# In feed-forwards x on the other side of the weights, 64 bytes off, and three gate units with weights at 256-byte multiples from x

## The chip, the core and the metric

The kernel runs on one core of a Trainium2 chip. The metric is the device time of one execution in microseconds (us). One execution was also taken with the hardware profiler; all rows below come from that one.

## What is computed

Two transformer blocks on 256 positions of width 1024, all in float32, one after the other. The first has a mixer (a gated delta rule and an S5 state space), a cross-attention and a SwiGLU feed-forward. The second has two layers, each with a self-attention (stick-breaking and MoBA heads in layer 0, forgetting attention in layer 1), a cross-attention to a memory, and a feed-forward with a short convolution over the positions. So there are three feed-forwards, of this form:

```python
def _swiglu(x, w_gate, w_up, w_down):
    return (silu(x @ w_gate) * (x @ w_up)) @ w_down      # 1024 -> 2816 -> 1024
def conv_ffn(h, w_up, conv_w, conv_b, w_down):
    c = conv_b + sum(up[:, i:i + S] * conv_w[i] for i in range(3))   # up = h @ w_up, padded in front
    return (silu(c[..., :2816]) * c[..., 2816:]) @ w_down
```

## The kernel before

**Products.** A float32 product is made of three products of rounded halves (mm3, and the same in out_mm): weight high by x high, weight high by x low, weight low by x high. The weights are the stationary operand (128x128, an LDWEIGHTS), x is the moving one (128x256), except in the V projections (proj_t), where x is stationary and the weights move. A unit of weights is 128x1024 numbers: 24 matmuls, 8 slices by three products.

**Weights.** The class Weights holds all units in the order of their use. load_ahead (L101) loads each from HBM into a raw tile. pump takes the next unit: ACT writes its rounded half into whi (L137) and, at the next pump, DVE writes the rest into wlo (L157). There are four pairs of whi and wlo tiles in the pool "weights", and from the first feed-forward on three more in the pool "weights2" (W.more). A unit takes one of the four if one is free, else one of the three, and gives it back when its last matmul has read it. So at most seven units are split at a time. step calls pump(1) after each unit of matmuls.

**Feed-forward.** ffn runs over 22 column blocks j: the gate unit (g), the up unit (u), and, two or three blocks later (LAG), the down unit (d) of an earlier block. Unit 0 of a feed-forward is g of j=0, so that g of j=8 is the 23rd unit used with LAG 2 and the 22nd with LAG 3. The last four down units are used together at the end. In the first feed-forward, "f0", rope_consts is called at j=4; it has one tiny matmul on TensorE (L1809). residual makes the next x out of the accumulated sums: it writes N.xh and N.xl, tiles of 8 slices of 256 numbers, sl and ahl hold the down product's moving operand, and N.rb a row scale that the readers of a projection multiply by.

**Addresses.** Tiles lie one behind the other in a partition's memory, pool behind pool. As laid out before, every whi and wlo tile starts 192 bytes behind a multiple of 256 (the first at byte 24,000), xh, xl and ahl 128 bytes behind one (xh at byte 69,248). A weight slice takes 512 bytes and a slice of x 1024, so the distance between two operands modulo 256 is the same for all slices. In what follows the **distance** of a matmul is the start of its moving operand minus the start of its stationary one, modulo 256. It is -64 for all products of a unit of weights with x, ahl or an attention's output as the moving operand. It is +64 in the V projections, where the roles are exchanged. It is 0 in the S5 gate (s5ghl by whi) and in the scores and the application of the first cross-attention (V, lb and K by Q, PT by xvh). These three are all that occur in long runs.

The tile v1 (192 bytes, at the start of the pool "main"), "beside" (128 bytes) and "beside2" (64 bytes) set these offsets.

Of the kernel before, what the change touches and what calls it, by code (L numbers as in the profile page):

```python
# [10 lines left out]
F32 = mybir.dt.float32  # L11
F32R = mybir.dt.float32r
# [7 lines left out]
S = 256  # L20
KD = D // 128
# [11 lines left out]

MEMORY = "s0 w1 s1 w1 s2 w1 s3 w1 v0 t0 w1 v1 t1 w1 p0 t2 w1 p1 x0 t3 w1 p2 p3 x1".split()

XK_AT = [("v", 1), ("z", 0), ("z", 1), ("z", 1)]
EPS = 1e-6
PI = math.pi
# [6 lines left out]
class Weights:  # L45
# [3 lines left out]
    def __init__(self, nc, pool, nraw, nsplit, behind):  # L49
        self.nc, self.pool, self.nraw, self.nsplit = nc, pool, nraw, nsplit  # L50
        self.plan, self.units, self.gain, self.gains = {}, [], {}, None
        self.loaded = 0
        self.raw, self.place, self.parts, self.where = {}, {}, {}, {}
        self.lo = self.more = None
        self.next = 0

        self.extra, self.nextra, self.once, self.spares, self.live = None, 0, False, [], {}
        self.lane = lambda k: nullcontext()
        self.hold, self.held, self.behind = None, 0, behind
# [53 lines left out]
    def pump(self, n=1):  # L113

        for _ in range(n):
            while self.next < self.loaded and not self.plan[self.units[self.next][0]][2]:
                self.next += 1
            if self.next >= len(self.units) or len(self.where) >= self.nsplit + (self.more[1] if self.more else 0):
                self.finish_lo()
                return False  # L120
            if self.next >= self.loaded:
                self.finish_lo()
            if self.next >= self.loaded:
                return False
            u = self.units[self.next]
            src = self.raw[u]
            shape = [128, int(src.shape[1]), int(src.shape[2])]
            used = list(self.where.values())
            at = int(used.count(0) == self.nsplit)
            pool, tag, bufs = (self.more[0], "2", self.more[1]) if at else (self.pool, "", self.nsplit)  # L130
            hi = pool.tile(shape, F32R, name="whi", tag="whi" + tag, bufs=bufs)
            lo = pool.tile(shape, F32R, name="wlo", tag="wlo" + tag, bufs=bufs)
            self.where[u] = at
            with self.lane("w"):
                g = self.gain[u[0]]
                if g is None:
                    i_ = self.nc.scalar.activation(hi, src, AF.Copy)  # L137
                else:
                    for k in range(shape[1]):
                        n = u[1] * shape[1] + k  # L140
                        i_ = self.nc.scalar.activation(hi[:, k], src[:, k], AF.Copy, scale=self.gains[g][:, n:n + 1])
            if self.held > 0:
                self.behind(i_.ins, self.hold[0])
            self.finish_lo()
            self.lo = (lo, src, hi, u)
            self.parts[u] = (hi, lo)
            self.next += 1
        return True
# [81 lines left out]
def body(ctx, tc, I, out):  # L230
# [5 lines left out]
    const = ctx.enter_context(tc.tile_pool(name="const", bufs=1))  # L236
    wpool = ctx.enter_context(tc.tile_pool(name="weights", bufs=1))
    main = ctx.enter_context(tc.tile_pool(name="main", bufs=1))
    small = ctx.enter_context(tc.tile_pool(name="small", bufs=2))
    W = Weights(nc, wpool, 4, 4, lambda a, b: behind(tc, a, b))  # L240

    v1 = main.tile([128, 48], F32, name="v1")


    def cols(w, c0, c1):
# [23 lines left out]
            W.order((nm, int(x[1])), c)  # L269

    def plan_ffn(tag, wg, g0, wu, u0, wd):
        for p in range(NH // 2):
            W.add((tag, "g", p), cols(wg, g0 + 256 * p, g0 + 256 * p + 256), order=False)
            W.add((tag, "u", p), cols(wu, u0 + 256 * p, u0 + 256 * p + 256), order=False)
            W.add((tag, "d", p), rows(wd, 2 * p), "k", order=False)
        lag = LAG[tag]
        for j in range(NH + lag):
            for c, jj in (("g", j), ("u", j), ("d", j - lag)):
                if 0 <= jj < NH:
                    W.order((tag, c, jj // 2), jj % 2)  # L280
# [115 lines left out]
    COL = W.gains = {}  # L396
# [64 lines left out]
    N = State()  # L461
# [1 line left out]
    N.by_feature = True  # L463
    N.last = None

    def new_x():
        N.xh = main.tile([128, KD, S], F32R, name="xh", tag="xh", bufs=1)
        N.xl = main.tile([128, KD, S], F32R, name="xl", tag="xl", bufs=1)

    def split_x(n, src, gcol):  # L470
        a = A.activation(N.xh[:, n], src[:, n], AF.Copy, scale=gcol)
# [5 lines left out]
    def finish_r(v):  # L477

        exp = A.set == A.SETS[AF.Exp]
        e = V if not late1 else A if exp or not N.by_feature else G  # L480
        late1.append(1)
        N.r = rsqrt_small(v, 2, e)
        if not N.by_feature:
            return
        p = acc()
        bcast_rows(p, N.r, 2)
        N.rb = main.tile([128, S], F32, name="rb", tag="rb", bufs=2)
        V.tensor_copy(N.rb, p[:, :S])

    def sum_rows(p, c0, sq):  # L490
# [92 lines left out]
        T.matmul(p, lhsT=wh[:, kk, c], rhs=xl, start=False, stop=False, skip_group_check=True)  # L583
        T.matmul(p, lhsT=wl[:, kk, c], rhs=xh, start=False, stop=last, skip_group_check=True)  # L584

    def residual(accs, gcol, fold=None, by_feature=True):


        h = hn = N.h
        N.by_feature = by_feature  # L590
        new_x()
        if fold is not None:
            gg = small.tile([128, KD], F32, name="gg", tag="gg", bufs=1)
            V.tensor_tensor(gg, gcol, fold, op=OP.mult)
            gcol = gg
# [28 lines left out]
        def first():  # L624
            p = acc()
# [15 lines left out]
            N.r = rr[:, 0:2]  # L641
            p = acc()
            bcast_rows(p, rr, 4)
            N.rb = main.tile([128, S], F32, name="rb", tag="rb", bufs=2)
            V.tensor_copy(N.rb, p[:, :S])

            def normed():
# [54 lines left out]

    N.h = hT = main.tile([128, KD, S], F32, name="h", tag="h", bufs=1)
    new_x()
    def transpose_in(dst, src, evac, bank):
        for kp in range(4):
            p = bank()
            pv = halves(p)
            for k2 in range(2):
                for t in range(2):  # L710
                    k = 2 * kp + k2
                    T.transpose(pv[:, k2, t * 128:(t + 1) * 128], src[t][:, k * 128:(k + 1) * 128], ident)
            evac(kp, pv)
# [8 lines left out]
    for n in range(KD):  # L722
        src, gcol = xb[n // 2][:, n % 2], COL["mix"][:, n:n + 1]
# [663 lines left out]
    for n in range(4):  # L1387
        p = mm()
# [5 lines left out]
        if n == 1:  # L1394
            split_x32()
        W.pump(1)
    fin_v(lambda i, n: v1[:, 0:n] if i else const.tile([128, n], F32, name="v0"))
    layer_cols()
    mixed = []

# [118 lines left out]


    pm = ctx.enter_context(tc.tile_pool(name="second", bufs=1))
    pm.tile([128, 32], F32, name="beside")
    kvT = pm.tile([128, 2, S], F32, name="kvT")
    kvv = pm.tile([128, 2, S], F32, name="kvv")

# [154 lines left out]
    for x in CROSS:  # L1680
        ops[x[0]](int(x[1]))
    mem2l = w_["mem2l"]
    residual(accs, COL["ffn"])
    px_cm.__exit__(None, None, None)
    W.more = (ctx.enter_context(tc.tile_pool(name="weights2", bufs=1)), 3)
    W.more[0].tile([128, 16], F32, name="beside2")
    padded = ctx.enter_context(tc.tile_pool(name="padded", bufs=1))
    W.nextra = 2
    W.extra = lambda: main.tile([128, 2048], F32, name="raw4", tag="m8", bufs=3)
# [20 lines left out]
    def ffn(tag, gcol, conv=None, fold=None):  # L1710
# [12 lines left out]
        def act(j, p):  # L1723
# [18 lines left out]
            s = pm.tile([128, S], F32, name="sl", tag="e3", bufs=6)  # L1742
            A.activation(s, t[:, 0], AF.Silu)
            tt(s, s, t[:, 1], OP.mult)
            a = pm.tile([128, 2, S], F32R, name="ahl", tag="e3", bufs=6)
            st.last = A.activation(a[:, 0], s, AF.Copy, keep=True).ins
            tt(a[:, 1], s, a[:, 0].bitcast(F32), OP.subtract)
            st.a[j] = (a[:, 0], a[:, 1])
# [270 lines left out]
    def memory_attention(l, gcol):  # L2019
# [39 lines left out]
            ops[x[0]](int(x[1]))  # L2059
        accs = [acc() for _ in range(4)]  # L2060
        out_last(accs, ("xao", l), w["o"], True)
        residual(accs, gcol)

    def fox_gates():

# [120 lines left out]
```

## Time and profile before

| | |
|---|---|
| median of 3 runs | 1190.58 us (1190.51 to 1200.14) |
| the profiled execution's own time | 1196.38 us |
| its span, first to last instruction | 1194.6 us |
| TensorE (PE) busy in it | 97% |
| VectorE (DVE), ScalarE (ACT) | 75%, 56% |

The time of an execution is its span and under 2 us around it. The busy share of PE is made of modelled ends, so it tells that PE is hardly ever without work, not how fast it works; how fast is read from the number of matmuls in a stretch.

### The profile page before, as it was taken

Reading aid. Unit: us, or ns where it says so; the run is one execution under the profiler, and the core shown is the slowest. Engines: PE = TensorE matmul, PEld = TensorE weight load, DVE = VectorE, ACT = ScalarE, POOL = GpSimd, SP = SyncE. Lnnn points to the kernel's source line nnn. Section 1 sums busy time; section 2 is a strip of 40 time slices with the busy share of each in tenths; the row PEclk is TensorE's granted clock in tenths of the full one; section 3 lists DMA queues with packets and bytes.
Section 4 is the critical chain, followed back from the end, with each engine's and each line's share of the span. In section 5 each row is a group of like instructions: output and inputs, shape, how many; then the busy total and the mean of one; then the engine's idle time right before and its main releaser. Section 6 shows DMA issues by size and latency. Waiting matters only on the chain.

```text
span 1194.6 us, 24101 instructions
## 1 busy us (share of the span) xinstructions
PE 1156.8 (97%) x9720; PEld 1102.7 (92%) x9720; DVE 891.8 (75%) x1682; ACT 667.1 (56%) x1155; POOL 77.1 (6%) x175
## 2 busy tenths in 40 slices
PE   8999998999999999999998999999999999999998
PEld 6798888999999999988797999999988888999998
DVE  8899747866875565877876899877765686978775
ACT  6553345655644444756665665655454666655653
POOL 1425300100000000200000000000100000000000
PEclk9999899999999999999999999999999999999998
DMA  8733352746665665653353576665543464666530
GB/s 207 198 83 109 98 159 63 220 150 188 194 198 169 195 198 163 185 169 118 105 168 113 162 208 194 195 212 158 145 140 116 143 172 137 179 190 195 176 90 36
DMA packets 262017, 188.01 MB, mean 157 GB/s; under 512 B 20143, under 2 KB 246852, under 8 KB 261906
## 3 DMA queue, kind: packets, MB, share of 16 engines
q1 hardware_dynamic: 258034, 185.23, 52.9%
q8 instruction: 76, 1.25, 0.4%
q10 hardware_dynamic: 3568, 0.86, 0.3%
q0 software_dynamic: 304, 0.39, 0.3%
q14 instruction: 35, 0.29, 0.1%
HBM read 183.70 MB, written 2.75 MB: 156 GB/s over the span
## 4 chain that ended last, share of the span: by engine, by line
PE 83%; DVE 7%; DMA 4%; ACT 2%; issue 1%; POOL 1%; SPq 0%; ACTq 0%; DVEq 0%; POOLq 0%
PE mm L536 16%; PE mm L537 16%; PE mm L538 16%; PE acc L582 7%; PE acc L584 7%; PE acc L583 7%; DVE wlo L157 1%; PE acc L1995 1%; DMA raw<-in_w_in_dram 1%; DVE s5a L747 1%; DVE ca L1110 1%; PE acc L1866 1%; DMA s5u<-uT 1%; DMA raws<-in_w_out_dram 1%; ACT whi L137 1%
## 5 line engine op out<-in xcount | busy, mean ns | idle before, releaser
L157 DVE TENSOR_TENSOR wlo<-raw,whi 128x1024 fp32r<-128x1024 f32 x322 | 392.0, 1226 | 149.6 <-ACT whi L137 147.3
L137 ACT ACTIVATE whi<-raw 128x1024 fp32r<-128x1024 f32 x322 | 337.0, 1057 | 285.6 <-PE mm L537 106.2
L536 PE MATMUL mm<-xh,whi 128*128 128x256 f32 x1504 | 421.3, 281 | 2.3 <-ACT V L218 1.4
L537 PE MATMUL mm<-xl,whi 128*128 128x256 f32 x1504 | 420.1, 280 | 0.0
L538 PE MATMUL mm<-xh,wlo 128*128 128x256 f32 x1504 | 419.7, 279 | 0.0
L536 PEld LDWEIGHTS mm<-xh,whi 128*128 128x128 f32 x1504 | 283.4, 189 | 4.3 <-ACT V L218 1.5
L537 PEld LDWEIGHTS mm<-xl,whi 128*128 128x128 f32 x1504 | 282.8, 188 | 1.5 <-issue 1.0
L538 PEld LDWEIGHTS mm<-xh,wlo 128*128 128x128 f32 x1504 | 283.6, 189 | 0.3
L584 PE MATMUL acc<-ahl,wlo 128*128 128x256 f32 x528 | 144.8, 279 | 0.4 <-DVE wlo L157 0.4
L583 PE MATMUL acc<-ahl,whi 128*128 128x256 f32 x528 | 144.9, 279 | 0.0
L582 PE MATMUL acc<-ahl,whi 128*128 128x256 f32 x528 | 141.7, 279 | 0.2 <-ACT ahl L218 0.2
L584 PEld LDWEIGHTS acc<-ahl,wlo 128*128 128x128 f32 x528 | 99.2, 189 | 0.8 <-DVE wlo L157 0.8
L583 PEld LDWEIGHTS acc<-ahl,whi 128*128 128x128 f32 x528 | 98.9, 188 | 0.0
L582 PEld LDWEIGHTS acc<-ahl,whi 128*128 128x128 f32 x528 | 97.2, 189 | 0.5 <-ACT ahl L218 0.5
L1740 DVE SCALAR_TENSOR_TENSOR gu<-pad,cwc,gu 128x256 f32<-128x256 f32 x176 | 75.1, 478 | 3.4 <-ACT gu L218 3.4
L582 PE MATMUL acc<-oh,whi 128*128 128x256 f32 x224 | 61.8, 284 | 0.9 <-ACT oh L218 0.9
L584 PE MATMUL acc<-oh,wlo 128*128 128x256 f32 x224 | 61.9, 279 | 0.0
L583 PE MATMUL acc<-ol,whi 128*128 128x256 f32 x224 | 61.7, 278 | 0.0
L218 ACT ACTIVATE gu<-pad,cwc 128x256 f32<-128x256 f32 x88 | 47.5, 590 | 14.7 <-DVE pad L747 14.6
L582 PEld LDWEIGHTS acc<-oh,whi 128*128 128x128 f32 x224 | 41.3, 188 | 2.5 <-ACT oh L218 1.9
L584 PEld LDWEIGHTS acc<-oh,wlo 128*128 128x128 f32 x224 | 42.1, 188 | 1.1 <-issue 1.1
L583 PEld LDWEIGHTS acc<-ol,whi 128*128 128x128 f32 x224 | 42.2, 188 | 0.4 <-issue 0.4
(537 smaller groups left out, 1951.7 us busy)
## 6 DMA issues: line engine op xcount, KB each, us to landing
raw<-in_ffn_w_up_dram SPq DMA_DIRECT2D x88, 512.0 KB
raw<-in_ffn_w_down_dram SPq DMA_DIRECT2D x44, 512.0 KB
raw<-in_ab_w_in_dram SPq DMA_DIRECT2D x24, 512.0 KB
raw<-in_fox_w_in_dram SPq DMA_DIRECT2D x24, 512.0 KB
raw<-in_w_gate_dram SPq DMA_DIRECT2D x22, 512.0 KB
raw<-in_w_up_dram SPq DMA_DIRECT2D x22, 512.0 KB
raw<-in_w_down_dram SPq DMA_DIRECT2D x22, 512.0 KB
raw<-in_w_in_dram SPq DMA_DIRECT2D x20, 512.0 KB
```

Source lines behind the costliest of these rows:

```text
L137: i_ = self.nc.scalar.activation(hi, src, AF.Copy)
L157: i_ = self.nc.vector.tensor_tensor(lo, src, hi.bitcast(F32), op=OP.subtract)
L218: i = self.nc.scalar.activation(out, in_, func, **kw)
L536: T.matmul(p, lhsT=wh, rhs=xh, start=start, stop=False, **kw)
L537: T.matmul(p, lhsT=wh, rhs=xl, start=False, stop=False, **kw)
L538: T.matmul(p, lhsT=wl, rhs=xh, start=False, stop=stop, **kw)
L582: T.matmul(p, lhsT=wh[:, kk, c], rhs=xh, start=first and n % 2 == 0, stop=False, skip_group_check=True)
L583: T.matmul(p, lhsT=wh[:, kk, c], rhs=xl, start=False, stop=False, skip_group_check=True)
L584: T.matmul(p, lhsT=wl[:, kk, c], rhs=xh, start=False, stop=last, skip_group_check=True)
L747: N.v = V.tensor_tensor(o, a, b, op=op).ins
L1110: STT(a, c[:, i:i + S], w(i), a, op0=OP.mult, op1=OP.add)
L1740: STT(t[:, i], u[:, i, d:d + S], cw(d, j + NH * i), t[:, i], op0=OP.mult, op1=OP.add)
```

## The change

Six parts, in the order of the diff.

- **Slots.** W.more now has two ordinary pairs instead of three, and a seventh pair (tag "3") that only the gate units of j = 1, 3 and 8 (APART) of each feed-forward take, when it is free. Two gaps of 64 bytes lie ahead of the two and ahead of the one.
- **x in one tile.** xh and xl are two parts of one tile of 16,384 + 128 bytes. The residuals ahead of the three feed-forwards put them 128 bytes further on (at=32), all others at its start.
- **ahl** likewise lies 128 bytes further on in its tile.
- **rb** has one buffer instead of two.
- **v1** goes from main to const, and a gap of its size stays in main. So everything from the weights on lies 192 bytes further on, weights and x alike.
- "gap1" (128 bytes) fills up what the 128 bytes of x's tile left of 256; "beside" is now "gap2".

By these sizes the distance of all products of a feed-forward becomes +64 instead of -64, apart from the nine APART gate units, where it is 0. Outside the feed-forwards all distances of products with weights stay as they were.

```diff
+APART = (1, 3, 8)
@@ pump
-            if self.next >= len(self.units) or len(self.where) >= self.nsplit + (self.more[1] if self.more else 0):
+            used = list(self.where.values())
+            if self.next >= len(self.units):
                 self.finish_lo()
                 return False
+            if self.more and self.units[self.next] in self.apart and 2 not in used:
+                at = 2
+            else:
+                at = int(used.count(0) == self.nsplit)
+                if at and (not self.more or used.count(1) == self.more[1]):
+                    self.finish_lo()
+                    return False
...
-            at = int(used.count(0) == self.nsplit)
-            pool, tag, bufs = (self.more[0], "2", self.more[1]) if at else (self.pool, "", self.nsplit)
+            pool = self.more[0] if at else self.pool
+            tag, bufs = (("", self.nsplit), ("2", 2), ("3", 1))[at]
@@ body
-    v1 = main.tile([128, 48], F32, name="v1")
+    main.tile([128, 48], F32, name="gap")
@@ plan_ffn
+        W.apart.update(((tag, "g", j // 2), j % 2) for j in APART)
...
-    def new_x():
-        N.xh = main.tile([128, KD, S], F32R, name="xh", tag="xh", bufs=1)
-        N.xl = main.tile([128, KD, S], F32R, name="xl", tag="xl", bufs=1)
+    def new_x(at=0):
+        t = main.tile([128, 2 * KD * S + 32], F32R, name="x", tag="x", bufs=1)
+        N.xh, N.xl = (t[:, at + i * KD * S:at + (i + 1) * KD * S].rearrange("p (k s) -> p k s", k=KD) for i in range(2))
...
-        N.rb = main.tile([128, S], F32, name="rb", tag="rb", bufs=2)
+        N.rb = main.tile([128, S], F32, name="rb", tag="rb", bufs=1)
...
-    def residual(accs, gcol, fold=None, by_feature=True):
+    def residual(accs, gcol, fold=None, by_feature=True, at=0):
...
-        new_x()
+        new_x(at)
...
+    main.tile([128, 32], F32, name="gap1")
...
-    fin_v(lambda i, n: v1[:, 0:n] if i else const.tile([128, n], F32, name="v0"))
+    fin_v()
...
-    residual(accs, COL["ffn"])
+    residual(accs, COL["ffn"], at=32)
     px_cm.__exit__(None, None, None)
-    W.more = (ctx.enter_context(tc.tile_pool(name="weights2", bufs=1)), 3)
-    W.more[0].tile([128, 16], F32, name="beside2")
+    W.more = (ctx.enter_context(tc.tile_pool(name="weights2", bufs=1)), 2)
+    W.more[0].tile([128, 16], F32, name="gap3")
+    for n in ("whi", "wlo"):
+        for i in range(2):
+            W.more[0].tile([128, 1024], F32R, name=n, tag=n + "2", bufs=2)
+    W.more[0].tile([128, 16], F32, name="gap4")
@@ act
-            a = pm.tile([128, 2, S], F32R, name="ahl", tag="e3", bufs=6)
+            a = pm.tile([128, 2 * S + 32], F32R, name="ahl", tag="e3", bufs=6)[:, 32:].rearrange("p (i s) -> p i s", i=2)
@@ memory_attention
-        residual(accs, gcol)
+        residual(accs, gcol, at=32)
```

## Rows read from the trace of the kernel before

**Rows 1.** The span and granted TensorE clock; busy time, share and instructions by engine.
```profile
core 0: 1194.6 us, clock 0.987
PE 1156.8 (97%) x9720; PEld 1102.7 (92%) x9720; DVE 891.8 (75%) x1682; ACT 667.1 (56%) x1155; POOL 77.1 (6%) x175
```

**Rows 2.** The chain that ended last, its shares of the span by engine.
```profile
PE 83%; DVE 7%; DMA 4%; ACT 2%; issue 1%; POOL 1%; SPq 0%; ACTq 0%; DVEq 0%; POOLq 0%
```

**Rows 3.** Windows, us from:to, length, busy (instructions) by engine; feed-forwards one, two, three.
```profile
336.00:480.00 144.00, 144.00 (x1223) 144.00 (x1224) 89.67 (x119) 65.31 (x91) 0.00 (x0) 1.00 0.61 181
670.00:826.00 156.00, 156.00 (x1377) 155.86 (x1376) 131.84 (x212) 93.65 (x144) 0.93 (x1) 1.00 0.66 193
1026.00:1177.00 151.00, 151.00 (x1284) 150.96 (x1282) 119.62 (x192) 85.86 (x130) 0.00 (x0) 1.00 0.52 156
```

**Rows 4.** Groups of matmuls in 336:480, then in 670:826; us busy, mean ns.
```profile
L536 PE MATMUL mm<-xh,whi 128*128 128x256 f32 x272 | 76.4, 281 | 0.0
...
L536 PE MATMUL mm<-xh,whi 128*128 128x256 f32 x303 | 83.6, 276 | 0.0
```

**Rows 5.** PE in order of time, 181.6 to 184: distance 0; first and last of 20.
```profile
181.64 0.28 PE L536 MATMUL mm<-s5ghl,whi 128*128 128x256 f32 x1
...
183.92 0.28 PE L536 MATMUL mm<-s5ghl,whi 128*128 128x256 f32 x1
```

**Rows 6.** Windows right behind distance 0, at distance -64.
```profile
243.90:249.50 5.60, 5.60 (x50) 5.60 (x49) 4.60 (x10) 2.99 (x8) 0.00 (x0) 1.00 0.63 187
258.50:264.10 5.60, 5.60 (x50) 5.60 (x49) 3.42 (x8) 2.26 (x5) 0.00 (x0) 1.00 0.43 134
```

**Rows 7.** Windows: V projections, distance +64, begun after a break on PE.
```profile
519.30:524.50 5.20, 5.20 (x46) 5.20 (x46) 5.16 (x12) 1.45 (x2) 0.00 (x0) 1.00 0.27 81
```

**Rows 8.** Windows: distance -64, then +64 without a break.
```profile
495.00:498.70 3.70, 3.70 (x35) 3.70 (x35) 3.70 (x4) 2.41 (x5) 1.90 (x2) 1.00 0.62 180
499.00:502.70 3.70, 3.70 (x35) 3.70 (x34) 2.69 (x4) 1.86 (x3) 1.82 (x2) 1.00 0.81 226
```

**Rows 9.** PE in order of time at 335.4: the tiny matmul of rope_consts.
```profile
335.61 0.38 PE L1809 MATMUL mm<-ones,invrow 1*128 1x1 f32 x2
```

**Rows 10.** Windows: the three feed-forwards in parts.
```profile
336.00:363.00 27.00, 27.00 (x230) 27.00 (x231) 20.99 (x35) 12.72 (x20) 0.00 (x0) 1.00 0.59 184
366.00:480.00 114.00, 114.00 (x970) 114.00 (x970) 66.94 (x83) 51.22 (x69) 0.00 (x0) 1.00 0.62 182
320.00:335.00 15.00, 15.00 (x135) 15.00 (x134) 10.91 (x18) 7.79 (x14) 1.59 (x33) 1.00 0.74 221
652.00:663.00 11.00, 11.00 (x99) 11.00 (x99) 9.47 (x16) 7.84 (x13) 0.00 (x0) 1.00 0.18 53
672.00:826.00 154.00, 154.00 (x1360) 153.86 (x1358) 129.96 (x210) 93.47 (x143) 0.93 (x1) 1.00 0.66 192
998.00:1008.00 10.00, 10.00 (x91) 10.00 (x90) 8.81 (x15) 6.89 (x12) 0.00 (x0) 1.00 0.17 52
1016.00:1025.00 9.00, 9.00 (x82) 9.00 (x81) 8.50 (x15) 5.78 (x10) 0.00 (x0) 1.00 0.33 99
1026.00:1057.00 31.00, 31.00 (x265) 30.98 (x264) 27.10 (x48) 18.47 (x30) 0.00 (x0) 1.00 0.73 223
1060.00:1176.00 116.00, 116.00 (x987) 116.00 (x987) 89.40 (x140) 64.69 (x96) 0.00 (x0) 1.00 0.47 141
```

**Rows 11.** What PE waited for, whole span: the one wait for a split.
```profile
PE acc L584 <- DVE wlo L157: 0.4, 1, 0.4
```

**Rows 12.** Groups of the splits; us busy, mean ns, idle before.
```profile
L157 DVE TENSOR_TENSOR wlo<-raw,whi 128x1024 fp32r<-128x1024 f32 x322 | 392.0, 1226 | 149.6 <-ACT whi L137 147.3
L137 ACT ACTIVATE whi<-raw 128x1024 fp32r<-128x1024 f32 x322 | 337.0, 1057 | 285.6 <-PE mm L537 106.2
```

More of the change, by code (lines that the diff above doesn't have):

```diff
@@ L54, in __init__ @@
         self.lo = self.more = None
+        self.apart = set()
         self.next = 0
@@ L127, in pump @@
             shape = [128, int(src.shape[1]), int(src.shape[2])]
-            used = list(self.where.values())
-            at = int(used.count(0) == self.nsplit)
-            pool, tag, bufs = (self.more[0], "2", self.more[1]) if at else (self.pool, "", self.nsplit)
+            pool = self.more[0] if at else self.pool
+            tag, bufs = (("", self.nsplit), ("2", 2), ("3", 1))[at]
             hi = pool.tile(shape, F32R, name="whi", tag="whi" + tag, bufs=bufs)
@@ L643, in first @@
             bcast_rows(p, rr, 4)
-            N.rb = main.tile([128, S], F32, name="rb", tag="rb", bufs=2)
+            N.rb = main.tile([128, S], F32, name="rb", tag="rb", bufs=1)
             V.tensor_copy(N.rb, p[:, :S])
@@ L1521, in body @@
     pm = ctx.enter_context(tc.tile_pool(name="second", bufs=1))
-    pm.tile([128, 32], F32, name="beside")
+    pm.tile([128, 32], F32, name="gap2")
     kvT = pm.tile([128, 2, S], F32, name="kvT")
```

## The prediction

> **What bounds the kernel now.** I read the shares by engine first: PE is busy 97% of the span, at a granted clock of 0.987 [rows 1]. The chain that ended last says the same: 83% of it is PE, no other engine over 7% [rows 2]. PE waited once, for 0.4 us, for a split of weights [rows 11]. So the time is the number of matmuls times the time from one start to the next, and that is read by counting matmuls in a stretch.
>
> The three feed-forwards do this in long unbroken runs, and not at one pace [rows 3]. In the first, 1223 matmuls take 144 us: 117.7 ns each. In the second, 1377 take 156 us: 113.3 ns. In the third, 1284 take 151 us: 117.6 ns. The granted clock is 1.00 in all three, the 2.4 GHz level, so the clock isn't the difference. The kind of matmul isn't either: it is the same line, with the same operands at the same distance (-64), and the records show 281 ns in one run and 276 in the other [rows 4]. I call the two **slow** and **fast**. They differ by 4.4 ns a matmul, and each holds for over 1200 matmuls, through gate, up and down products. A break on PE can change it: at 335.6 us a tiny matmul comes between [rows 9], the stretch ahead of it is fast (15 us, 135 matmuls) and that behind it slow [rows 10]. So the same program can run each feed-forward at either pace. One whole feed-forward is worth some 1377 x 4.4 = 6.1 us, close to what lies between the profiled execution (1196.38) and the median (1190.58).
>
> **What the traces show of the distance.** At distance 0 there is one pace only: 19 steps from 181.64 to 183.92 are 120 ns each [rows 5]. At -64 and at +64 both paces occur, and changing from -64 to +64 without a break keeps a run fast (35 matmuls in 3.7 us on both sides) [rows 8]; in the trace this holds 7 times of 7 for fast, 3 of 3 for slow. What a run comes out of decides its pace. Out of distance 0 into -64 without a break it was slow 9 times of 9, if more than two matmuls stood at 0 (5.6 us for 50 matmuls, two or three of them cut by the window's edges) [rows 6]. Out of a break into -64 it was fast 41 times and slow 24 times. Out of a break into +64 it was slow 15 times of 16 (46 matmuls in 5.2 us) [rows 7]. Distance 0 into +64 does not occur in the trace. That is the step on which this change hangs.
>
> **The change part by part.** Sum against the profiled execution's own 1196.38 us.
>
> *Distance +64 in feed-forwards.* By itself it gains nothing: pace is carried over, and out of a break it is worse than -64, slow rather than fast. I count all matmuls of a feed-forward ahead of the first clean passage through distance 0 as slow. The g unit of j=1 is used mixed with those of j=0, so I take j=3 as the first clean one (321, 669 and 1018 us). In the second feed-forward 99 matmuls from 652 to 663 turn slow, in the third 91 from 998 to 1008 [rows 10]: 190 x 4.4 = **0.8 us lost**. The first was mostly slow there.
>
> *Nine units at distance 0.* 216 matmuls at 120 ns. Where the run was fast, 6.7 ns more each, where it was slow, 2.3: the first feed-forward has one of three in a fast stretch, the second all three, the third two; 6 x 24 x 6.7 + 3 x 24 x 2.3 = **1.1 us lost**.
>
> *What follows them.* Bounds: fast (113.3 ns) or slow (117.7 ns). The nearest row is distance 0 into -64, always slow [rows 6]. I don't take its value but its opposite, and this is the choice on which the forecast rests: out of a break the two signs go opposite ways, -64 mostly fast, +64 nearly always slow, so what one sign does on being entered, the other seems to reverse; out of distance 0, -64 goes slow, so +64 should go fast. Then everything behind the unit of j=8 is fast to the end of the feed-forward. In the first, j=8 ends at 366 us: 970 matmuls [rows 10], 4.3 us. In the third it ends at 1060: 987 matmuls, 4.3 us. In the second they are fast already. **8.6 us gained.** Between j=3 and j=8 I count nothing: the tiny matmul at 335.6 [rows 9] and a short interruption at 1026 come after j=3, and out of a break +64 is slow, as these stretches are now (230 and 265 matmuls, 27 and 31 us [rows 10]). If j=3 carried through, 495 x 4.4 = 2.2 us more.
>
> *Slots.* Ordinary units have six pairs instead of seven. At the end of a feed-forward four down units are held, so two units of the self-attention behind it can be split ahead instead of three; the third is split when the four are given back, while ACT and DVE write the new x. It is hidden by the matmuls of the two that are ready (48 x 113 ns = 5.4 us against 1.06 + 1.23 us of a split [rows 12]). If that cover is gone, one split is in the open at each of two places: 2 x 2.3 = 4.6 us. From below it cannot gain, PE waited only 0.4 us in all for splits [rows 11]. I take 0. Inside the feed-forwards the APART unit has its own pair, so as many are in flight as before; a slot is refilled in the time of a unit (2.7 us) and takes 2.3.
>
> *The rest.* The sole rb is rewritten only after a whole projection has used the old one; x in one tile is written after the same matmuls as before, since xh and xl are read together; ahl's tile grows inside a larger slot; the first writes into the new pairs wait for nothing. No instruction is added on any engine or queue, no DMA is moved. With 192 bytes more in front, distances to the constants change, as in transposes, which showed no difference by distance. 0, at most 1 us either way.
>
> Sum: -8.6 + 1.1 + 0.8 = -6.7; 1196.4 - 6.7 = **1189.7 us**, 0.1% under the median. The median's executions may have had another mix of paces than the profiled one; the nine units should make it the same one each time.
>
> **Rivals.**
>
> *A, slower: distance 0 goes slow into +64 as well.* For it: the only entry out of 0 that the trace has goes slow, 9 of 9. Against it: the opposite behaviour of the signs out of a break. Its place is the up unit behind each APART unit, and it decides at the first one. Then all is slow: 135 matmuls in the first feed-forward, 99 + 1360 in the second, 91 + 82 in the third [rows 10], 1767 x 4.4 = 7.8 us, and 216 x 2.3 = 0.5 at distance 0: 1204.7 us, 1.2% over the median.
>
> *B, the splits come late.* The 4.6 us above on top of the forecast: 1194.3. The 0.4 us wait speaks against it.
>
> *C, the change doesn't do what it says: the distance has no part in the pace, and breaks draw it.* For it: both paces occur at one distance. Against it: 120 ns at distance 0 only, 15 of 16 and 9 of 9. Then the time stays where it was, 1190.6 to 1196.4 us, as the draws fall. The Trainium skill has a rule that would make this so, in "TensorE: Matmul & The Clock Gate", section "Part 2: What happens when you issue a matmul": the array has separate read ports for moving operand and weights, so that loading the next weights takes no read bandwidth from the running matmul. By that rule, where x lies can't matter and C is right; the trace disagrees in so far as the pace at distance 0 was 120 ns and never 113.
>
> **How the numbers follow.** Forecast 0.60, A 0.17, B 0.08, C 0.15. Around the forecast the sum can come out 2.2 us lower (j=3 carries through), 0.8 lower (no slow starts) and 1 either way (the rest): 1185.7 to 1190.7. And some of the 5.8 us between the profiled execution and the median may be no pace at all; taken off the median instead, the same 6.7 us give 1183.9. That is the lower end, 1183.5. With B (1194.3) and C (up to 1196.4, and 1 us for the rest) the range reaches up to 1198; A stays outside. About 1% (11.9 us) is what a measurement can tell from no change. Slower means over 1202.5: nearly all of A, 0.15. Faster means under 1178.7, which no case gives: 0.02. Within 1%: 0.83.
>
> **What would show it.** In the three feed-forwards of the changed kernel, behind the g unit of j=8: 113.3 ns a matmul and records of 276 ns if I am right, 117.7 and 281 if A is. Three stretches of 24 matmuls at 120 ns in each feed-forward. A start of the second and third at 117.7. If the feed-forwards keep one fast and two slow, or vary from run to run, it is C. If PE waits for whi or wlo at the start of the self-attentions, B. I am wrong, too, if other breaks behind j=8 make a run slow again.

## The result, and the profile after

The changed kernel took 1208.66 us, the median of six executions (1206.0 to 1211.22), the kernel before on the same chip 1193.56 (1189.94 to 1200.14): a ratio of 1.012, 95% interval 1.0081 to 1.016. It is slower by 1.2%; 1189.7 was predicted. The profiled executions stand at 1206.54 and 1196.38: 10.2 us to explain.

The page of the changed kernel opens as the one before did [rows 1], only longer:

```profile
span 1204.7 us, 24113 instructions
PE 1167.5 (97%) x9720; PEld 1113.6 (92%) x9720; DVE 892.5 (74%) x1682; ACT 667.4 (55%) x1155; POOL 77.6 (6%) x175
```

PE is still what bounds the time, and it runs the same 9720 matmuls. So I count matmuls in stretches again, as in [rows 3, 10]. Windows of the changed kernel, with the same columns as there: the first feed-forward, the second, the third, and then each behind its gate unit of j=8.

```profile
336.00:480.00 144.00, 144.00 (x1225) 144.00 (x1224) 88.15 (x117) 65.23 (x91) 0.00 (x0) 1.00 0.61 182
677.00:835.00 158.00, 158.00 (x1344) 158.00 (x1343) 130.03 (x208) 91.96 (x141) 0.93 (x1) 1.00 0.61 181
1037.00:1188.00 151.00, 150.50 (x1312) 150.10 (x1311) 122.08 (x195) 88.33 (x134) 0.00 (x0) 1.00 0.52 156
366.00:480.00 114.00, 114.00 (x970) 114.00 (x970) 65.64 (x82) 50.05 (x68) 0.00 (x0) 1.00 0.59 176
718.00:835.00 117.00, 117.00 (x996) 117.00 (x995) 91.55 (x141) 64.83 (x96) 0.00 (x0) 1.00 0.61 182
1078.00:1180.00 102.00, 102.00 (x903) 102.00 (x902) 81.53 (x126) 59.80 (x88) 0.00 (x0) 1.00 0.52 156
```

Behind j=8 the first feed-forward is slow as before (970 in 114 us), the second has turned slow (996 in 117 us, 117.5 ns; before, 1360 in 154 us), and only the third is fast (903 in 102 us, 113 ns). The granted clock is 1.00 in all of them.

The other loss is in the two memory attentions. Longest waits of PE, first the kernel before, then the changed one:

```profile
PE mm L1588 <- DVE P L1548: 3.9, 2, 2.0
```

```profile
PE mm L1602 <- DVE P L1562: 7.9, 2, 4.0
```

Subtracting the start of the same matmul in the two traces at the stage borders gives where the 10.2 us arose: first feed-forward +0.4, memory attention 0 +2.6, second feed-forward +6.6, memory attention 1 +2.6, third up to j=8 +1.5, behind j=8 -4.1, together 9.6; the rest is spread over the other stages.

### The profile page after: what moved, and what is told of

The parts are those of the page before. It is cut to its first block, busy times and chain, and to the rows that moved or that the text cites. A ratio compares the mean times of both kernels' runs of the same rounds, so it can differ in the third digit from the quotient of the medians.

```text
span 1204.7 us, 24113 instructions
## 1 busy us (share of the span) xinstructions
PE 1167.5 (97%) x9720; PEld 1113.6 (92%) x9720; DVE 892.5 (74%) x1682; ACT 667.4 (55%) x1155; POOL 77.6 (6%) x175
## 4 chain that ended last, share of the span: by engine, by line
PE 83%; DVE 8%; DMA 3%; ACT 2%; issue 1%; SPq 1%; POOL 1%; ACTq 0%; DVEq 0%; POOLq 0%
PE mm L549 17%; PE mm L550 17%; PE mm L551 17%; PE acc L597 7%; PE acc L595 7%; PE acc L596 7%; DVE wlo L168 1%; DMA raw<-in_w_in_dram 1%; PE acc L1884 1%; DVE s5a L761 1%; PE acc L2013 1%; DVE ca L1124 1%; DVE s5z L978 1%; DMA s5u<-uT 1%; ACT whi L148 1%
## 5 line engine op out<-in xcount | busy, mean ns | idle before, releaser
L549 PE MATMUL mm<-x,whi 128*128 128x256 f32 x1504 | 421.6, 281 | 1.3 <-ACT x L229 0.9
L550 PE MATMUL mm<-x,whi 128*128 128x256 f32 x1504 | 420.2, 280 | 0.0
L551 PE MATMUL mm<-x,wlo 128*128 128x256 f32 x1504 | 420.2, 280 | 0.0
L549 PEld LDWEIGHTS mm<-x,whi 128*128 128x128 f32 x1504 | 282.4, 188 | 3.0 <-ACT x L229 1.1
L550 PEld LDWEIGHTS mm<-x,whi 128*128 128x128 f32 x1504 | 282.8, 188 | 1.1 <-issue 0.8
L551 PEld LDWEIGHTS mm<-x,wlo 128*128 128x128 f32 x1504 | 282.5, 188 | 0.5 <-issue 0.2
```

Of the source, the lines that this page charges most:

```text
L549: T.matmul(p, lhsT=wh, rhs=xh, start=start, stop=False, **kw)
L550: T.matmul(p, lhsT=wh, rhs=xl, start=False, stop=False, **kw)
L551: T.matmul(p, lhsT=wl, rhs=xh, start=False, stop=stop, **kw)
```

## The passage through distance 0

PE of the changed kernel in order of time, at the start of the gate unit of j=8 in the first feed-forward (start, duration):

```profile
363.55 0.28 PE L597 MATMUL acc<-ahl,wlo 128*128 128x256 f32 x1
363.67 0.28 PE L549 MATMUL mm<-x,whi 128*128 128x256 f32 x1
363.79 0.28 PE L550 MATMUL mm<-x,whi 128*128 128x256 f32 x1
363.90 0.29 PE L551 MATMUL mm<-x,wlo 128*128 128x256 f32 x1
364.03 0.28 PE L549 MATMUL mm<-x,whi 128*128 128x256 f32 x1
364.15 0.28 PE L550 MATMUL mm<-x,whi 128*128 128x256 f32 x1
364.26 0.28 PE L551 MATMUL mm<-x,wlo 128*128 128x256 f32 x1
```

This is not the steady 120 ns of [rows 5]. In the trace's nanoseconds the steps are 120, 120, 125, 117, 118, and again, to the end of the 24: the mean is 120, but a pattern of five runs through, and behind it the run is slow as ahead of it. In the second feed-forward it is the same. In the third the run enters behind a single step of 115 ns, settles to the steady 120 and comes out fast. That gave the theory to test. (One unit never was at distance 0: in the second feed-forward j=3 found the seventh pair in use by j=1 and ran at +64, with no step of 120 ns between 669 and 715 us. So there are eight such units, not nine, and j=8 is the first clean one there.)

**Theory M.** Distance 0 does not reset a run; it carries the phase between the two operand streams through (a picture: the traces show steps, no phase), unless an interruption comes right ahead of it. After an interruption it settles to the steady 120 ns, and +64 behind that is fast. **Rival A**, from the prediction: distance 0 into +64 is slow in itself. **Rival C** (D in the expectations below): breaks draw the pace, the distance has no part. **Theory S**, for the memory attentions: six pairs in place of seven; its rival is the one buffer of rb, or x and its low half in one tile.

## The experiments

In the profile fences of this section each line is a window of 40 us inside the part behind j=8 of one feed-forward, in their order, unless the text says otherwise: about 342 matmuls in it is slow, 355 is fast (the window's edges add two or three).

**Seven pairs, nothing at distance 0** (e1_seven).

```
-APART = (1, 3, 8)
+APART = ()
-W.more = (... "weights2" ..., 2)      # and its tiles, bufs=2
+W.more = (... "weights2" ..., 3)      # and its tiles, bufs=3
```

> The changed kernel with x and ahl at +64 in the feed-forwards, no units at distance 0, and seven ordinary pairs of weight tiles again. Theory M (a run of matmuls keeps its pace until a break, and +64 out of a break is slow): all three feed-forwards slow, 117.7 ns a matmul, also the third behind j=8, which the changed kernel ran fast (971 matmuls, +4.3 us); theory S (the 2.6 us that each memory attention lost came from the seventh pair, through the order of the work): both memory attentions go back, the wait for P at its transpose in memory attention from 7.9 to about 3.9 us, -5.2 us. Both together: 1206.5 + 4.3 - 0.5 - 5.2 = 1205 us. If S is wrong: 1210. Rival D (the pace is drawn anew at each break, whatever the distance): about half of the feed-forwards fast, 1194 to 1200.

It took 1207.72 us. All three feed-forwards are slow, here the second:

```profile
740.00:780.00 40.00, 40.00 (x342) 40.00 (x341) 31.94 (x51) 22.92 (x34) 0.00 (x0) 1.00 0.68 187
```

And its wait of PE for P:

```profile
PE mm L1602 <- DVE P L1562: 3.9, 2, 2.0
```

It is 3.9 us again, with rb and x's tile as in the changed kernel. So both of S's rivals fall. (The time is 2.7 us over the 1205 expected; the first down unit starts at 332.4 us instead of 326.0.) What the pair does can be seen on DVE, first in the changed kernel, then here:

```profile
630.42 0.69 DVE L1550 TENSOR_REDUCE nm<-acc 128x2 f32<-128x512 f32 x1 [0.15 <-PE acc L1595]
...
631.09 0.69 DVE L1550 TENSOR_REDUCE nm<-acc 128x2 f32<-128x512 f32 x1
...
631.97 0.68 DVE L1550 TENSOR_REDUCE nm<-acc 128x2 f32<-128x512 f32 x1
...
632.76 0.30 DVE L761 TENSOR_TENSOR nm<-nm,rs 128x2 f32<-128x2 f32 x3
```

```profile
637.13 0.69 DVE L1550 TENSOR_REDUCE nm<-acc 128x2 f32<-128x512 f32 x1 [0.50 <-PE acc L1595]
...
637.94 0.16 DVE L761 TENSOR_TENSOR nm<-nm,rs 128x2 f32<-128x2 f32 x1
638.01 0.68 DVE L1550 TENSOR_REDUCE nm<-acc 128x2 f32<-128x512 f32 x1
```

With seven pairs the first head's maximum is scaled 0.8 us after its reduction began, so its exponential can start. With six, the order on DVE has three reductions ahead of the first scaling, 2.3 us after, and every P is late. Of the row scale, which the scaling needs (L450 to L453, L1585), four steps stand between these reductions; with seven pairs only the last one comes behind the first reduction. PE then waits 4.0 us instead of 2.0, and behind the wait it runs at half the clock; the changed kernel's PE, and a window over it:

```profile
635.33 0.47 PE L1602 MATMUL mm<-ident,P 128*128 128x128 f32 x1 [3.98 <-DVE P L1562]
...
636.03 0.41 PE L551 MATMUL mm<-whi,mem2l 128*128 128x256 f32 x1
636.24 0.41 PE L549 MATMUL mm<-whi,mem2h 128*128 128x256 f32 x1
```

```profile
632.00:640.00 8.00, 4.67 (x23) 4.67 (x23) 3.59 (x15) 3.35 (x9) 0.00 (x0) 0.64 0.44 130
```

Starts are 0.21 us apart there instead of 0.11 to 0.12, at a granted clock of 0.64 over these 8 us (part of them at the 1.2 GHz level); in this run with seven pairs it is 1.00 at that place. The half clock is not new with the change, though. In the kernel before, the 8 us around the same wait, of 2.0 us there, show 0.79:

```profile
629.60:637.60 8.00, 6.04 (x40) 5.59 (x37) 5.53 (x16) 3.48 (x10) 0.00 (x0) 0.79 0.62 197
```

Over all traces here, steps of 213 ns followed 10 of 10 waits of 4.0 us and 9 of 18 waits of 2.0 us. In the changed kernel 22 of the 40 steps behind either wait are of that kind, in the kernel before 14 and 17: with the 2.0 us of waiting, that makes about the 2.6 us.

**A break ahead of distance 0** (e2_break_kick), in the changed kernel:

```
             p = mm()
+            if j in (1, 3, 8):
+                T.matmul(p[:, 0:1], lhsT=ones[0:1, :], rhs=ones[0:1, 0:1], start=True, stop=True)
             proj_f(p[:, :S], (tag, "g", j // 2), j % 2)
```

> The changed kernel with one tiny matmul (1x128 by 1x1) ahead of the gate unit of j=8 in each feed-forward (and one each for j=1 and j=3, which land in the first matmuls of the stage). It breaks the run directly ahead of the 24 matmuls at distance 0. Theory M: after the break these settle at a steady 120 ns and the run that follows at +64 is fast in all three feed-forwards: 113.3 ns for some 970 to 1000 matmuls each, 1206.5 - 4.3 - 4.4 + 1 = 1199 us. Rival D: pace drawn, no better than the changed kernel's one of three; 1203 to 1207. Rival A' (distance 0 goes slow into +64 and the third feed-forward was an accident): all three slow, 1211.

All three feed-forwards are fast behind j=8:

```profile
380.00:420.00 40.00, 40.00 (x355) 40.00 (x354) 24.40 (x30) 18.96 (x25) 0.00 (x0) 1.00 0.59 177
740.00:780.00 40.00, 40.00 (x356) 40.00 (x355) 32.77 (x52) 24.41 (x36) 0.00 (x0) 1.00 0.74 212
1100.00:1140.00 40.00, 40.00 (x355) 40.00 (x354) 31.84 (x50) 23.89 (x35) 0.00 (x0) 1.00 0.64 190
```

Each unit at j=8 begins with steps near 210 and 220 ns and settles to 120. A and C both fall: A says distance 0 goes slow, C that distance 0 is not needed (see the next run). The time was 1205.45, not the 1199 expected. This execution was 4.1 us late already at 291 us, ahead of the first feed-forward, and a break costs 0.5 us (steps of 209, 133, 175 and 220 ns in place of two of 118), nine of them 4.5 where the expectation had 1: 1206.5 - 4.3 - 4.4 + 4.1 + 4.5 = 1206.4.

**The break alone** (e3_break_only): the same, and APART = ().

> The same tiny matmuls without any unit at distance 0: gate units of j=1, 3, 8 are at +64 like the others. Theory M: out of a break +64 is slow (15 of 16 before), so all three feed-forwards stay slow behind j=8, 117.7 ns: 1206.5 + 4.3 + 1 - 0.5 = 1211 us. Rival B' (the break alone sets the pace): fast behind j=8 in all three, as in the kernel with distance 0, about 1199.

1215.53 us, slow in all three (342 in each window). One of them:

```profile
740.00:780.00 40.00, 40.00 (x342) 40.00 (x342) 31.34 (x49) 23.34 (x35) 0.00 (x0) 1.00 0.67 196
```

A break into +64 is slow, as in [rows 7]; break and distance 0 are both needed.

**Other distances** (e4_dist_a): six pairs, nothing at distance 0, x and ahl at -32 in the first feed-forward, +32 in the second, 128 in the third.

> No units at distance 0, no tiny matmuls, six pairs; x and ahl at distance -32 in the first feed-forward, +32 in the second, 128 in the third. What the traces show so far is 120 ns at 0, 113.3 or 117.7 at 64 on either side. Theory M, if the pace falls with the distance from 0: 32 on either side lies between, 113 to 120, with a step inside a feed-forward only at a break; 128 at 113.3. Rival D, the distance has no part: 113.3 or 117.7 in each, nothing else. A third value, or one value without any slow stretch at 128, speaks against D. Time 1195 to 1213.

1219.49 us. By step in the traces: 118.3 ns at -32, 117.8 at +32, 118.7 at 128; no fast stretch. The time lies above the 1195 to 1213 expected, and 128 did not run at 113.3. Steps of 118.3 and 118.7 ns occur at ±64 in no long run, which speaks against C. None of these did better than ±64; each was tried in one feed-forward, from one entry.

**The pair opened to the attentions** (e5_free_slot):

```
-APART = (1, 3, 8)
+APART = (8,)                     # and the one-column matmul ahead of j=8
                 if at and (not self.more or used.count(1) == self.more[1]):
-                    self.finish_lo()
-                    return False
+                    if not self.more or 2 in used or self.units[self.next][0][0] in ("f0", "f1", "f2"):
+                        self.finish_lo()
+                        return False
+                    at = 2
```

> The changed kernel with APART = (8,), the one-column matmul ahead of the gate unit of j=8 only, and the pair of the distance-0 unit open to the units of the attentions when the six ordinary pairs are taken (so they have seven, as before the change). Theory S (what the memory attentions lost, 2 x 2.6 us, comes from six pairs in place of seven): PE's longest wait for P is 2.0 us, as before the change, not 4.0; each memory attention gets its 2.6 us back. Theory M (a break right ahead of distance 0 makes it the steady 120 ns, and +64 behind it fast): 113.3 ns behind j=8 in all three feed-forwards. Both: 1206.5 - 5.2 - 4.3 (first FF) - 4.4 (second) = 1192.6 us. S alone wrong: waits of 4.0 and about 1198. Rival: the loss in the memory attentions comes from the one buffer of rb or from x and its low half in one tile, which stay: waits of 4.0.

S and M both hold: PE's wait for P is 3.9 us in two waits of 2.0, and all three are fast (355, 356, 356). 1200.58 us, 8 over the estimate: 5.0 us in the part up to the first down unit (331.0 instead of 326.0), and at the end of the second feed-forward a wait of 2.2 us for a split wlo, with a granted clock of 0.83 behind it (830 to 840 us).

**A second passage, entered fast and unbroken** (e6_second_passage): APART = (8, 13), the one-column matmul ahead of j=8 only.

> As e5_free_slot, with a second gate unit at distance 0, j=13, that has no one-column matmul ahead: it is entered at 113.3 ns (fast), unbroken. Theory M (distance 0 carries the phase it was entered with through, unless broken): from fast it runs with another pattern than the five-step one, and what comes out is not settled by M. Rival 1 (an unbroken passage always leaves slow): 117.8 ns behind j=13, some 650 matmuls x 3 x 4.4 ns = 8 us more than e5_free_slot, 1201. Rival 2 (a fast run stays fast through it): 113.3 behind j=13 and 1193.

1195.54 us. The entry of j=13 in the first feed-forward, and then windows behind j=13 in each:

```profile
407.80 0.28 PE L599 MATMUL acc<-ahl,wlo 128*128 128x256 f32 x1
407.91 0.28 PE L551 MATMUL mm<-x,whi 128*128 128x256 f32 x1
408.03 0.28 PE L552 MATMUL mm<-x,whi 128*128 128x256 f32 x1
408.15 0.28 PE L553 MATMUL mm<-x,wlo 128*128 128x256 f32 x1
408.27 0.28 PE L551 MATMUL mm<-x,whi 128*128 128x256 f32 x1
408.39 0.28 PE L552 MATMUL mm<-x,whi 128*128 128x256 f32 x1
```

```profile
412.00:452.00 40.00, 40.00 (x355) 40.00 (x355) 23.97 (x29) 18.16 (x25) 0.00 (x0) 1.00 0.64 187
757.00:797.00 40.00, 40.00 (x355) 40.00 (x355) 31.14 (x48) 23.14 (x34) 0.00 (x0) 1.00 0.60 181
1108.00:1148.00 40.00, 40.00 (x355) 40.00 (x354) 31.12 (x48) 23.27 (x34) 0.00 (x0) 1.00 0.54 155
```

Out of a fast stretch distance 0 is steady from its first step, and what follows stays fast, 3 of 3: the second rival. So the same distance, at the same mean step of 120 ns, can let out at either pace. Unbroken, it mostly let out the one that came in: 113.3 ns after 113.3 here, 117.8 after 117.8 in most passages of the changed kernel (counted below).

**The kernel before with one break** (e7_before_break): only the one-column matmul ahead of j=8.

> The kernel before with nothing but the one-column matmul ahead of the gate unit of j=8: x stays at -64, no unit at distance 0. In the trace before, runs at -64 behind an interruption came out fast 41 times and slow 24. Theory D (the pace at -64 is drawn anew at an interruption, fast in about two of three): behind j=8 each of the three feed-forwards is fast or slow independently of what it ran before, most likely two of three fast; time 1188 to 1198. Rival (the draw at -64 is not changed by so short a break): the pace behind j=8 is the pace ahead of it in all three.

```profile
380.00:420.00 40.00, 40.00 (x355) 40.00 (x355) 24.73 (x30) 18.98 (x25) 0.00 (x0) 1.00 0.61 186
740.00:780.00 40.00, 40.00 (x342) 40.00 (x341) 31.36 (x48) 23.08 (x34) 0.00 (x0) 1.00 0.67 192
1100.00:1140.00 40.00, 40.00 (x355) 40.00 (x355) 32.02 (x50) 23.66 (x35) 0.00 (x0) 1.00 0.61 181
```

1193.64 us. At -64 the break turned all three: slow, fast, slow ahead of it, fast, slow, fast behind. The rival falls. Whether it is a draw or always a turn, three cases don't say; elsewhere in this trace an interruption by four small matmuls, with nearly the same first and last step (206 and 223 ns, at 864 us), left the pace at 113.3 ns.

**Second executions of both kernels** (e8_after_again, e12_before_again), nothing edited.

> The changed kernel as it is, another execution. If the pace that comes out of an unbroken passage through distance 0 at j=8 is drawn from execution to execution (the runs' times form two groups, 1206.0 to 1206.7 and 1210.7 to 1211.2, 4.6 us apart, about one feed-forward's 971 matmuls x 4.4 ns = 4.3), the number of feed-forwards that are fast behind j=8 is one (1206) or none (1211). If it is fixed by the program, the third is fast again, the first and second slow, and the groups come from elsewhere.

> The kernel before as it is, another execution. If its time's spread (1187.5 to 1202.8 in the runs beside e9 and e10) is the pace drawn for each feed-forward at -64 plus the part up to the first feed-forward (which in the executions traced so far reached its first down unit 0 to 7 us later than in the first trace of before), then the three feed-forwards show another mix than slow, fast, slow, or the first one begins later, and the time is 1196.4 less 4.4 ns for each matmul that turned fast, plus 4.4 for each that turned slow, plus the later start, within 2 us. If the mix is fixed by the program, it is slow, fast, slow again.

The changed kernel took 1213.63 us: the passage at j=8 shows the five-step pattern in all three feed-forwards, and all three are slow. With the first trace that makes, at j=8, five of six slow entries that came out slow, and the sixth is the one behind the 115 ns step.

Two other units show that M is too simple. The j=1 unit of the first feed-forward, entered slow and unbroken, came out fast in the first execution (behind two steps of 117 ns in a row) and slow in the second. And in the third feed-forward two matmuls for the row scale (L469) interrupt the run three matmuls ahead of the j=3 unit; here the first execution, and a window behind the unit:

```profile
1027.17 0.59 PE L469 MATMUL acc<-diag,ones 128*128 128x256 f32 x2
1031.00:1036.00 5.00, 5.00 (x45) 5.00 (x44) 4.77 (x11) 2.72 (x6) 0.00 (x0) 1.00 0.40 129
```

The unit ran the five-step pattern all the same and came out slow (117.8 ns), in both executions. In e2 the same interruption came six matmuls ahead of it, and it settled to 120 ns and came out fast; where it falls inside the j=3 unit (first feed-forward, both executions of the changed kernel) it did so too. So not every interruption near distance 0 sets the run. What is shown to set it is the one-column matmul directly ahead of the unit.

The kernel before took 1199.16 us and was slow, fast, slow again (342, 355, 342 in the windows), so its mix did not change, and of my expectation the other mix falls. What moved was the part ahead of the feed-forwards, by 2.9 us at 320 us. Windows 180 to 205 us, the first and the second execution of the kernel before (the granted clock is the third number from the end):

```profile
180.00:205.00 25.00, 21.82 (x172) 20.26 (x171) 17.12 (x45) 12.73 (x20) 0.00 (x0) 1.00 0.21 64
```

```profile
180.00:205.00 25.00, 21.81 (x148) 19.70 (x148) 16.48 (x44) 10.97 (x18) 0.00 (x0) 0.86 0.21 64
```

In the second, 24 fewer matmuls of the same program fit into the 25 us, at a clock of 0.86 instead of 1.00, behind the same two waits of 1.5 and 1.7 us. In the changed kernel's second execution it was 0.89, and PE's wait for mem was 5.0 us instead of 1.2; it reached the first down unit 4.7 us later than the first. Of the 7.1 us between its two profiled executions this is 4.7, and the slow third feed-forward 4.2 (161.7 instead of 157.5 us); some 1.7 came back in the stages between. So between these two executions pace makes 4.2 of 7.1 us in the changed kernel and nothing in the kernel before.

**Two breaks and two units at distance 0** (e9_two_kicks): e5_free_slot with j in (4, 8) in both places.

> e5_free_slot with APART = (4, 8) and a one-column matmul ahead of both gate units. Theory M, a pace set by hand: 113.3 ns from j=4 in the second and third feed-forward and from j=8 in the first (whose one-row matmul at j=5, the normalization's, breaks between), in every execution, so that the runs agree more closely with one another than those of the kernel before (1189.9 to 1200.1). About 260 matmuls x 4.4 ns = 1.1 us in each of two feed-forwards off the 1200.6 us of e5_free_slot: 1198; without the 2.2 us wait for wlo at the end of the second feed-forward and the half clock behind it (some 4 us there), 1194. Rival (the pace is drawn at the start of each execution as well): slow behind j=4 or j=8 in at least one feed-forward, and runs spread as widely as those of the kernel before.

M holds: all six passages settle to 120 ns and come out fast. Median of 12 executions 1197.4 us (1194.53 to 1201.09) beside 1195.15 of the kernel before (22 executions, 1187.53 to 1202.76): 1.0026 (1.0000 to 1.0051). The runs lie closer together than those of before (6.6 us in 12 executions, 15.2 in 22), as expected; that this comes from the pace set is not shown, since one of them was traced, and the kernel before kept its mix of paces in both of its traces.

**The pair opened to later units too** (e10_open_pair): the condition of e5_free_slot holds in a feed-forward only for `self.units[self.next][0][2] < 5`, so that units of j=10 and on may take the pair of the distance-0 unit when no other is free.

> e9_two_kicks with the pair of the distance-0 unit open to every unit behind j=9 of a feed-forward too, so that no stage has fewer than seven pairs. Theory S (fewer pairs is what made PE wait 2.2 us for wlo at the end of the second feed-forward in e3, e4, e5 and e6, against 0.4 with seven): the wait is 0.4 again; about 1193 us, 0.3% under the kernel before (median 1193.6 to 1196.3). The units that take the pair run at distance 0 too, some 24 matmuls x 7 ns each at most. Rival: the wait stays at 2.2, since it is the unit at distance 0 that is split late and not the number of pairs.

1197.33 us, 1.0030 (1.0011 to 1.0050). The edit changed nothing: no such unit comes to need the pair, and the kernel's instructions are those of e9, one for one. So this is e9 once more (2.3 us of wait for wlo at the end of the second feed-forward, 2.4 there), and the expectation is not tested by it. What the wait comes from stays open. The number of pairs at that place alone is not it, for e2 and e3 have six ordinary pairs each: it is 0.4 in the changed kernel, in e1 and in e2, and over 2 in e3, e4, e5, e6, e9, e10 and e11.

**Distance -64 with a break on both sides** (e11_both_breaks): e10 with x and ahl back at -64, gap4 48 numbers wide, and a one-column matmul ahead of the up unit too.

> e10_open_pair with x and ahl back at -64 in the feed-forwards (as before the change), the pair of j=4 and j=8 moved so that it lies at distance 0 from it, and a one-column matmul on both sides of that gate unit: ahead of its first matmul and ahead of the up unit's. In the traces distance 0 ran into -64 slow, 9 of 9 before the change, and in e7 a one-column matmul turned a slow run at -64 fast twice and a fast one slow once. Theory P (the break ahead sets the phase at distance 0 to the same steady 120 ns each time, so a break behind it starts -64 in one and the same way each time): all passages of the three feed-forwards come out alike. Alike and fast: the first feed-forward fast from j=8, the others from j=4, the attentions at -64 as before the change (114 to 115 ns, 2.0 and 1.4 us less than in e10): 1197.2 - 3.4 = 1193.8, 0.3% under the runs of before at the same start. Alike and slow: about 1204. Rival (a break at -64 draws, 41 to 24): some fast, some slow.

```profile
380.00:420.00 40.00, 40.00 (x355) 40.00 (x355) 24.40 (x30) 18.99 (x25) 0.00 (x0) 1.00 0.61 185
740.00:780.00 40.00, 40.00 (x356) 40.00 (x355) 32.61 (x51) 23.53 (x35) 0.00 (x0) 1.00 0.68 191
1100.00:1140.00 40.00, 40.00 (x356) 40.00 (x355) 31.89 (x50) 23.90 (x35) 0.00 (x0) 1.00 0.64 191
```

P holds: all six passages start -64 with the same steps to within 1 ns (222, 117, 117, 123, 118, then 113 and 114) and stay fast. The time does not follow: 1202.6 us, 1.0066 (1.0035 to 1.0097). Its first down unit stands at 334.1 us, 7.2 later than in the first trace of before, and the wait for wlo is 3.3 us. No version here is shown to beat the kernel before (e6 and e7, one execution each, took 0.7 and 2.6 us less than one of it beside them, well inside its spread); the program of e9 and e10 beats the changed kernel (1.003 against 1.012).

## Why the prediction was wrong, point by point

- *"Out of distance 0, -64 goes slow, so +64 should go fast."* This step failed. The second half held behind a one-column matmul: 21 of 21 passages with one directly ahead came out fast (three each in e2, e5 and e6, at j=8, six each in e9 and e10, which are one program), and out of a fast run (3 of 3 in e6). The changed kernel has no break at j=8, its runs arrive there slow and unbroken, and distance 0 passed the slow pace on, 5 times of 6. The rows that I had [rows 5, 6] showed distance 0 only in its steady form, and I took that for its one form ("at distance 0 there is one pace only"): the mean is one, the pattern isn't. The same trace had another entry to see: at 255.3 us distance 0 begins with steps of 127, 118, 125, 113 and 119 ns. Of the 8.6 us the first feed-forward gave nothing, the third 4.1.
- *"In the second they are fast already."* This is the largest error. Behind a break +64 is slow [rows 7], so runs start slow in a feed-forward, which I counted for 99 matmuls, up to j=3; since nothing reset it (j=3 was not at distance 0 there, j=8 passed it on), it held for the whole feed-forward: 341 matmuls from 675 us to j=8 and 996 behind it, together +6.6 us with what the start lost.
- *Slots, taken as 0, bounded by 4.6 us.* They cost 2 x 2.6 us, but not where I looked. No split came into the open at the start of the self-attentions; with one pair fewer the order on DVE in the memory attentions changed, PE waited 2.0 us longer in each, and a longer stretch at half the clock behind the wait took the rest. I had checked what waits for a pair, not what takes the place of a split that can't be issued.
- *Distance 0 as such* (1.1 us for 216 matmuls; it was eight units, 192) and *the slow starts* had the right sign; where runs are slow, distance 0 costs 24 x 2.2 ns a unit, next to nothing.
- *Rival A* had nearly the time of the first execution (1204.7), and the pace of two feed-forwards of three; its mechanism was wrong, as e2 shows. *Rival C* had the larger part of the spread for pace, which e12 does not bear out.
- Sum by the measured terms: 0.4 + 6.6 - 2.6 + 5.2 = 9.6, where -2.6 is the third feed-forward, against 10.2 measured and -6.7 predicted.

Not shown: why a stretch at 117.8 ns mostly keeps its pace through distance 0, what the 115 ns step is, and why the interruption three matmuls ahead of j=3 did not set the run. The lowest executions of before (1189.94 beside the changed kernel, 1187.53 beside e9) were not traced; 6.4 and 8.9 us under the first trace would fit one or two feed-forwards turned fast (4.3 us each behind j=8), but that is argued only.

## What to carry to other kernels

Where the same instruction shows two paces at full clock, ask what the run came out of, and look at the sequence of single steps, not at their mean: two patterns with one mean can lead to different ends. An element that should set a state needs an entry that is the same each time; test it entered from both states before building on it. Look whether an edit changed the instructions at all before reading its time. When a buffer is given up, compare the order of instructions of every stage that used it, the quiet ones too.

## What the runs showed of the hardware

- At distance 0 the step is 120 ns on average in two forms: steady (entered fast, or directly behind a one-column matmul), or 120, 120, 125, 117, 118 (entered slow and unbroken at j=8, 5 of 6; also 2 of 2 with an interruption three matmuls ahead).
- Two one-column matmuls around 24 matmuls at distance 0 set -64 fast 6 of 6 (e11), one directly ahead of it sets +64 fast 21 of 21. A pace thus set held through some 970 matmuls.
- In the memory attentions, waits of 4.0 us were followed by matmuls 213 ns apart 10 times of 10 (granted clock of 0.64 over 8 us around one), waits of 2.0 us at the same place 9 times of 18 (0.79 in the kernel before, 1.00 in e1).
- The same program, twice: clock 1.00 and 0.86 over the same 25 us behind the same two waits of 1.5 and 1.7 us; it cost 2.8 us.
